# One hybrid encoder step on one core: the down projection's 2x2 block product formed from seven products instead of eight

## The chip, the core and the metric

One NeuronCore of a Trainium2 chip runs the whole step; the other cores are idle. The metric is the device time of one execution in microseconds (us). The engines named below are TensorE (PE in the profile, its weight loads PEld), VectorE (DVE), ScalarE (ACT), GpSimd (POOL) and SyncE (SP), whose queue issues most DMAs.

## The reference, cut to what matters

Two layers process 512 prompt tokens and 32 sample tokens of width 1024. Each layer has a mixer (differential attention and a gated spatial unit), cross-attention to 256 memory tokens, and a feed-forward block with a causal convolution over three tokens. The change is in the last of these:

```python
def conv_ffn(h, hist, w_up, conv_w, conv_b, w_down):
    S = h.shape[1]
    g, up = jnp.split(h @ w_up, 2, axis=-1)          # 1024 -> 2 x 2816
    gp = jnp.concatenate([hist, g], axis=1)
    c = conv_b + sum(conv_w[j] * gp[:, j:j + S] for j in range(CONV_W))
    a = jax.nn.silu(c) * up
    return a @ w_down, gp[:, -(CONV_W - 1):]         # 2816 -> 1024
```

## The kernel before

Features stand on partitions and tokens on the free axis: 546 token columns, which are 512 prompt tokens, 2 columns of padding that carry the sample's convolution history, and 32 sample tokens (`T`, `S0`). One fp32 value is held as a hi part plus a lo part, and each product is three matmuls: hi by hi, hi by lo and lo by hi. `proj_fm` (L263) issues them for each k tile of 128 rows, each in two token parts of 256 and 290 columns (`NSPL`) into two PSUM banks, a and b. Its outputs are `pfg` and `pfu` (gate and up), `pfd` (down), `pq`, `pwo`, `pwc` and `pu` in the other stages.

Weights arrive as a stream of units. `emit_unit` loads a unit into `raw` (three buffers, L130), ACT copies the hi part (L133) and DVE subtracts to get the lo part (L134) into one of four `hl` buffers. `pop` keeps the units up to i + 3 emitted when unit i is used. So the splitting runs ahead of PE by one pair of units.

The feed-forward block of a layer runs in two halves of 11 feature tiles. Per feature tile there is a gate tile and an up tile, each 48 matmuls. DVE scales them by `rbc` (L910, L929), ACT and DVE do the convolution and the activation (L914 to L930), and `split` makes hi and lo of the result `at` (L173, L174). After 11 tiles the down projection runs over eight output tiles `ct`: 33 pairs of matmuls each, then `update_x` adds both banks to the residual `x` (L209). In the second half `after(ct)` follows each of them: in layer 0 `set_h`, which makes the gained hi and lo parts `hx` of the residual (L189, L190) and adds its squares into `ssq` (L196 on ACT, L201 on POOL); in layer 1 `final_x`, which transposes and stores the output.

PSUM has four banks under the tag R, two under S and two under B; `psR2` takes a pair from R, R or S in turn. The order of the instructions on each engine is fixed when the program is built: by place in the program among what is taken to be ready. Engines take their instructions strictly in that order.

## Time and profile before

| | us |
|---|---|
| median of 3 runs | 1721.8 (1720.87 to 1721.93) |
| span of the profiled execution | 1721.5 |
| PE busy | 1700.7 (99%) |
| DVE busy | 996.2 (58%) |
| ACT busy | 728.9 (42%) |
| POOL busy | 220.3 (13%) |

The span runs from the first to the last instruction of the profiled execution. No other time is given for that execution; the median of the runs is 0.3 us above its span. Busy time of PE counts a matmul until its modelled end, so that matmuls overlap: what a matmul costs is the distance from its start to the next one's start, not its duration.

### The profile page before, as it was taken

How to read it: one execution, taken by the hardware profiler on the slowest of the kernel's cores; microseconds unless marked ns; L12 is line 12 of the kernel's file. 1: busy time of each engine (PE TensorE's matmuls, PEld its weight loads, DVE VectorE, ACT ScalarE, POOL GpSimd, SP SyncE). 2: the span in 40 equal slices, each digit the busy share in tenths (PEclk: the TensorE clock that was granted, in tenths of full speed). 3: DMA queues.
4: the chain of work that ended last, by engine and by line, in shares of the span. 5: the costliest groups of instructions: out<-in, count | busy, mean ns of one | idle time of the engine just before them, and what ended most of it. 6: DMA issues, size and time to landing. Idle time of an engine off the chain costs nothing.

```text
span 1721.5 us, 32408 instructions
## 1 busy us (share of the span) xinstructions
PE 1700.7 (99%) x13115; PEld 1641.7 (95%) x13115; DVE 996.2 (58%) x2138; ACT 728.9 (42%) x1485; POOL 220.3 (13%) x624
## 2 busy tenths in 40 slices
PE   7999999999999999999999999999999999999998
PEld 6988899999999999999998888999999999999998
DVE  6778765565466624655367677655555665255642
ACT  5456754455333312333345576445543332133321
POOL 4000014221200000000111000422221000000000
PEclk9999999999999999999999999999999999999999
DMA  5222233442222233223332222243422322333131
GB/s 174 89 86 71 66 102 100 141 130 82 86 79 88 70 88 108 86 68 87 93 117 70 76 69 85 85 130 105 129 81 74 99 62 86 101 94 90 55 115 57
DMA packets 200988, 158.03 MB, mean 92 GB/s; under 512 B 8670, under 2 KB 200038, under 8 KB 200838
## 3 DMA queue, kind: packets, MB, share of 16 engines
q1 hardware_dynamic: 200774, 155.82, 29.8%
q8 instruction: 103, 1.69, 0.4%
q14 instruction: 47, 0.39, 0.1%
q10 hardware_dynamic: 64, 0.14, 0.0%
HBM read 144.83 MB, written 11.10 MB: 91 GB/s over the span
## 4 chain that ended last, share of the span: by engine, by line
PE 95%; ACT 1%; POOL 1%; DVE 1%; issue 1%; SPq 1%; DMA 0%; ACTq 0%; DVEq 0%
PE pfgb L263 8%; PE pfub L263 8%; PE pfdb L263 8%; PE pfua L263 7%; PE pfga L263 7%; PE pfda L263 7%; PE pr L282 4%; PE pr L280 4%; PE pr L281 4%; PE pwob L263 3%; PE pqb L263 3%; PE pwcb L263 3%; PE pwoa L263 3%; PE pwca L263 3%; PE pqa L263 3%; PE pub L263 2%
## 5 line engine op out<-in xcount | busy, mean ns | idle before, releaser
L134 DVE TENSOR_TENSOR hl<-raw,hl 128x1024 fp32r<-128x1024 f32 (+2 forms) x280 | 317.1, 1133 | 278.0 <-ACT hl L133 277.6
L133 ACT CAST hl<-raw 128x1024 fp32r<-128x1024 f32 (+2 forms) x280 | 269.9, 964 | 408.8 <-PE pfdb L263 139.2
L263 PE MATMUL pfgb<-hx,hl 128*128 128x290 f32 x1056 | 269.6, 297 | 0.0
L263 PE MATMUL pfdb<-at,hl 128*128 128x290 f32 x1056 | 269.5, 298 | 0.0
L263 PE MATMUL pfga<-hx,hl 128*128 128x256 f32 x1056 | 269.3, 283 | 0.0
L263 PE MATMUL pfda<-at,hl 128*128 128x256 f32 x1056 | 268.4, 282 | 0.0
L263 PE MATMUL pfub<-hx,hl 128*128 128x290 f32 x1056 | 264.9, 297 | 0.0
L263 PE MATMUL pfua<-hx,hl 128*128 128x256 f32 x1056 | 264.2, 283 | 0.5 <-ACT rbc L253 0.5
L263 PEld LDWEIGHTS pfdb<-at,hl 128*128 128x128 f32 x1056 | 200.4, 190 | 0.1
L263 PEld LDWEIGHTS pfgb<-hx,hl 128*128 128x128 f32 x1056 | 200.4, 190 | 0.0
L263 PEld LDWEIGHTS pfda<-at,hl 128*128 128x128 f32 x1056 | 200.0, 189 | 0.0
L263 PEld LDWEIGHTS pfga<-hx,hl 128*128 128x128 f32 x1056 | 199.6, 189 | 0.0
L263 PEld LDWEIGHTS pfub<-hx,hl 128*128 128x128 f32 x1056 | 198.3, 190 | 0.0
L263 PEld LDWEIGHTS pfua<-hx,hl 128*128 128x128 f32 x1056 | 196.9, 189 | 0.7 <-ACT rbc L253 0.7
L282 PE MATMUL pr<-hl,hx 128*128 128x256 f32 x512 | 147.8, 290 | 2.4 <-DVE hx L190 2.4
L280 PE MATMUL pr<-hl,hx 128*128 128x256 f32 x512 | 147.5, 289 | 1.4 <-DVE vs L305 0.9
L281 PE MATMUL pr<-hl,hx 128*128 128x256 f32 x512 | 147.6, 289 | 0.8 <-DVE hl L134 0.8
L282 PEld LDWEIGHTS pr<-hl,hx 128*128 128x128 f32 x512 | 98.0, 192 | 5.8 <-DVE hx L190 2.8
L281 PEld LDWEIGHTS pr<-hl,hx 128*128 128x128 f32 x512 | 98.3, 192 | 3.6 <-issue 1.7
L280 PEld LDWEIGHTS pr<-hl,hx 128*128 128x128 f32 x512 | 98.0, 192 | 3.7 <-DVE vs L305 1.1
L263 PE MATMUL pwcb<-co,hl 128*128 128x290 f32 x384 | 88.7, 298 | 0.0
L917 DVE SCALAR_TENSOR_TENSOR ct<-gb,cols,ct 128x546 f32<-128x546 f32 x88 | 69.3, 787 | 33.2 <-ACT ct L914 31.6
(360 smaller groups left out, 3312.7 us busy)
## 6 DMA issues: line engine op xcount, KB each, us to landing
raw<-in_w_up_dram SPq DMA_DIRECT2D x80, 512.0 KB
raw<-in_w_down_dram SPq DMA_DIRECT2D x32, 512.0 KB
raw<-in_w_in_dram SPq DMA_DIRECT2D x24, 512.0 KB
raw<-in_w_in_dram SPq DMA_DIRECT2D x32, 256.0 KB
raw<-in_w_out_dram SPq DMA_DIRECT2D x32, 256.0 KB
raw<-in_wq_c_dram SPq DMA_DIRECT2D x16, 512.0 KB
raw<-in_wk_c_dram SPq DMA_DIRECT2D x16, 512.0 KB
raw<-in_wv_c_dram SPq DMA_DIRECT2D x16, 512.0 KB
```

The source lines that it names most:

```text
L133: act.copy(hl[:, 0, 0:n * wc], raw[:, 0:n * wc])
L134: vec.tensor_tensor(out=hl[:, 1, 0:n * wc], in0=raw[:, 0:n * wc], in1=f32(hl[:, 0, 0:n * wc]), op=ALU.subtract)
L263: pe.matmul(out=ps[0 if n0 == 0 else 1][:, 0:nn], lhsT=hl[:, wpart, kk, col * 128:col * 128 + 128], rhs=mv[:, n0:n0 + nn], start=first and ...
L280: pe.matmul(out=out, lhsT=lh(k), rhs=hl[:, 0, k % 4], start=(k == 0), stop=False)
L281: pe.matmul(out=out, lhsT=lh(k), rhs=hl[:, 1, k % 4], start=False, stop=False)
L282: pe.matmul(out=out, lhsT=ll(k), rhs=hl[:, 0, k % 4], start=False, stop=(k == k8 - 1))
L917: vec.scalar_tensor_tensor(out=ct, in0=gb[:, jj:jj + T], scalar=c["cw"][:, jj, f:f + 1], in1=ct, op0=ALU.mult, op1=ALU.add)
```

## The change

The down projection is cut into 2 by 2 blocks: k tiles by even and odd, output tiles by first and second of a pair, tokens by first and second half of 272. Eight block products become seven (the Winograd form of Strassen's algorithm). The sums of weight blocks S1 to S4 are made on POOL in `emit_item`, from the raw weights; the sums of activation blocks T1 to T4 on POOL in `ffn_pair`. Then ACT and DVE make hi and lo parts of the seven weight blocks and of the seven activation blocks. `seven` issues a product after the other, three banks in all, and adds each product's bank to `x` when it ends; later products go on accumulating on the same bank.

The 22 feature tiles are 11 pairs in three parts of 3, 4 and 4 pairs, instead of two halves of 11 tiles. One pair of the next part is computed ahead of each part's down projection, save the last. The padding columns go: 544 columns in two parts of 272, and the sample's first two convolution outputs are corrected by small instructions on POOL and DVE. Weights are loaded in blocks of eight k tiles by 256 columns into two `raw` buffers, and split into eight operands of 4 KB a partition: hi and lo are tiles of their own, and a down block's hi and lo share one. Buffers shrink for it: `skq` and `vs` from two to one, and `cv` shares the one buffer of `ck`.

```diff
-HF = NF // 2
+PARTS = ((0, 3), (3, 7), (7, 11))
...
-T = 546          # tokens on the free axis: 512 prompt, 2 of padding, 32 sample
-S0 = 514         # first sample token
-NSPL = ((0, 256), (256, 290))
+T = 544
+S0 = 512
+TH = T // 2
+NSPL = ((0, TH), (TH, TH))
...
+    blocks, items = [], []
+    ORDER = ("A11", "A12", "S2", "S1", "S3", "S4", "A22")
...
+        def block(tag, loads, nk, seven=False):
+            blocks.append((loads, nk))
+            b = len(blocks) - 1
+            if seven:
+                for it in ORDER:
+                    items.append((tag, b, it))
+            else:
+                for k0 in range(0, nk, 4):
+                    items.append((tag, b, k0))
...
-            for hf in range(2):
-                for f in range(hf * HF, hf * HF + HF, 2):
-                    w = 128 * min(2, hf * HF + HF - f)
...
-                for ct in range(8):
-                    for k0, n in ((0, 8), (8, HF - 8)):
-                        units.append((f"dn{hf}_{ct}", [ks(a["w_down"][l][:, 128 * ct:128 * ct + 128],
-                                                          hf * HF + k0, n)], n, 128))
...
+            def gen(i):
+                two(f"g{i}", a["w_up"][l], [(256 * i, 256)])
+                two(f"up{i}", a["w_up"][l], [(FF + 256 * i, 256)])
+            gen(0)
+            for q, (p0, p1) in enumerate(PARTS):
+                for i in range(p0 + 1, min(p1 + 1, NF // 2)):
+                    gen(i)
+                nk = 2 * (p1 - p0)
+                for j in range(4):
+                    mat = a["w_down"][l][:, 256 * j:256 * j + 256]
+                    block(f"dn{q}_{j}", [(k0, min(4, nk - k0), 0, 256, ks(mat, 2 * p0 + k0, min(4, nk - k0)))
+                                         for k0 in range(0, nk, 4)], nk, seven=True)
...
-        raw = wp.tile([128, 1024], F32, tag="raw", bufs=3, name="raw")
...
-        hl = wp.tile([128, 2, 1024], F32R, tag="hl", bufs=4, name="hl")
-        act.copy(hl[:, 0, 0:n * wc], raw[:, 0:n * wc])
-        vec.tensor_tensor(out=hl[:, 1, 0:n * wc], in0=raw[:, 0:n * wc], in1=f32(hl[:, 0, 0:n * wc]), op=ALU.subtract)
...
+    def load(b):
+        while state["loaded"] <= min(b, len(blocks) - 1):
+            loads, nk = blocks[state["loaded"]]
+            raw = wp.tile([128, 2048], F32, tag="raw", bufs=2, name="raw")
+            rv = raw[:, 0:nk * 256].rearrange("p (k c) -> p k c", c=256)
+            for k0, kn, c0, cn, src in loads:
+                sp.dma_start(out=rv[:, k0:k0 + kn, c0:c0 + cn], in_=src)
+            raws[state["loaded"]] = rv
+            state["loaded"] += 1
+    def hilo(n):
+        return [wp.tile([128, 1024], F32R, tag="hl", bufs=SLOTS, name="hl")[:, 0:n] for _ in range(2)]
...
+    def emit_item(i):
+        tag, b, it = items[i]
+        load(b + 1)
+        raw, nk = raws[b], blocks[b][1]
+        if isinstance(it, int):
+            kn = min(4, nk - it)
+            hi, lo = hilo(kn * 256)
+            src = raw[:, it:it + kn].rearrange("p k c -> p (k c)")
+            act.copy(hi, src)
+            vec.tensor_tensor(out=lo, in0=src, in1=f32(hi), op=ALU.subtract)
+            wt[i] = tuple(v.rearrange("p (k c) -> p k c", c=256) for v in (hi, lo))
...
+        n = nk // 2
+        q = raw.rearrange("p (k e) (c n) -> p e c k n", e=2, c=2)
+        A11, A12, A21, A22 = q[:, 0, 0], q[:, 1, 0], q[:, 0, 1], q[:, 1, 1]
+        def summed(name, in0, in1, op):
+            t = tmp([128, 4, 128], name, tag="c2", bufs=3)[:, 0:n]
+            pool.tensor_tensor(out=t, in0=in0, in1=in1, op=op)
+            sums[name] = t
+        if it == "A11":
+            summed("S1", A21, A22, ALU.add)
+            summed("S2", sums["S1"], A11, ALU.subtract)
+        elif it == "A12":
+            summed("S3", A11, A21, ALU.subtract)
+        elif it == "S3":
+            summed("S4", A12, sums["S2"], ALU.subtract)
+        src = {"A11": A11, "A12": A12, "A22": A22}.get(it)
+        if src is None:
+            src = sums[it]
+        hl = wp.tile([128, 2, 4, 128], F32R, tag="hl", bufs=SLOTS, name="hl")[:, :, 0:n]
+        act.copy(hl[:, 0], src)
+        vec.tensor_tensor(out=hl[:, 1], in0=src, in1=f32(hl[:, 0]), op=ALU.subtract)
         wt[i] = hl
...
+    def cost(i):
+        return 2 if isinstance(items[i][2], int) else 1
+    def prefetch(slots=SLOTS):
+        while state["emitted"] < len(items) and state["held"] + cost(state["emitted"]) <= slots:
+            emit_item(state["emitted"])
+            state["held"] += cost(state["emitted"])
...
+        for i in state.pop("done", ()):
+            state["held"] -= cost(i)
         i = state["popped"]
-        prefetch(i + 4)
+        prefetch()
...
+        state["done"] = range(i, i + n)
...
                 pe.matmul(out=pb[:, 128 * t:128 * t + 128], lhsT=ones, rhs=dg[:, 2 * i + t], start=True, stop=True)
             if i == 1:
                 pe.matmul(out=pb[:, 256:288], lhsT=ones[0:32], rhs=dgs, start=True, stop=True)
-                act.copy(rbc[:, S0:T], pb[:, 256:288])
-            act.copy(rbc[:, 256 * i:256 * i + 256], pb[:, 0:256])
+            act.copy(rbc[:, 256 * i:256 * i + 256 + 32 * i], pb[:, 0:256 + 32 * i])
...
-                                  lhsT=hl[:, wpart, kk, col * 128:col * 128 + 128],
+                                  lhsT=hl[wpart][:, kk, col * 128:col * 128 + 128],
...
-        zs = tmp([32, 256], name, tag="vs" if name == "vs" else "zs", bufs=2)
+        zs = tmp([32, 256], name, tag="vs" if name == "vs" else "zs", bufs=1 if name == "vs" else 2)
...
-        skq = tmp([128, 352], "skq", tag="skq", bufs=2)
+        skq = tmp([128, 352], "skq", tag="skq", bufs=1)
...
-        cv = tmp([128, 2, 128], "cv", tag="cv", bufs=1)
+        cv = tmp([128, 2, 128], "cv", tag="ck", bufs=1)
...
+    def ffn_pair(l, i, rbc, fc, cnt, slots):
...
+            gs = tiny([128, 4], "gs")
+            ge = tiny([128, 2], "ge")
+            pool.tensor_copy(gs[:, 0:2], c["st"][:, :, f])
+            pool.tensor_copy(gs[:, 2:4], gb[:, S0 + 2:S0 + 4])
+            pool.tensor_scalar(out=ge, in0=gs[:, 2:4], scalar1=c["cw"][:, 2, f:f + 1],
+                               scalar2=c["cb"][:, f:f + 1], op0=ALU.mult, op1=ALU.add)
...
+            vec.scalar_tensor_tensor(out=ge, in0=gs[:, 1:3], scalar=c["cw"][:, 1, f:f + 1], in1=ge,
+                                     op0=ALU.mult, op1=ALU.add)
+            vec.scalar_tensor_tensor(out=ct[:, S0:S0 + 2], in0=gs[:, 0:2], scalar=c["cw"][:, 0, f:f + 1],
+                                     in1=ge, op0=ALU.mult, op1=ALU.add)
...
+        h0, h1 = slice(0, TH), slice(TH, T)
+        (sB, sT, sU, sD), d = slots
+        ts = G("t4", [128, 4, TH], "ts")
+        pool.tensor_tensor(out=ts[:, 0], in0=us[0][:, h1], in1=us[0][:, h0], op=ALU.subtract)
+        pool.tensor_tensor(out=ts[:, 1], in0=us[1][:, h1], in1=ts[:, 0], op=ALU.subtract)
+        pool.tensor_tensor(out=ts[:, 2], in0=us[1][:, h1], in1=us[0][:, h1], op=ALU.subtract)
+        pool.tensor_tensor(out=ts[:, 3], in0=us[1][:, h0], in1=ts[:, 1], op=ALU.subtract)
+        dv = sD[:, :, d * TH:d * TH + TH]
+        split(dv[:, 0], dv[:, 1], us[0][:, h0])
+        split(sB[:, 0], sB[:, 1], us[1])
+        for k, t in enumerate((sT, sU)):
+            split(t[:, 0], t[:, 1], ts[:, 2 * k:2 * k + 2].rearrange("p j t -> p (j t)"))
+        bl = {"B11": dv, "B21": sB[:, :, h0], "B22": sB[:, :, h1], "T1": sT[:, :, h0], "T2": sT[:, :, h1],
+              "T3": sU[:, :, h0], "T4": sU[:, :, h1]}
+        return bl, cnt
...
+    SEVEN = (("A11", "B11", 0, True, (0, 0)), ("A12", "B21", 1, True, (0, 0)), ("S2", "T2", 0, False, (0, 1)),
+             ("S1", "T1", 2, True, (1, 1)), ("S3", "T3", 0, False, (1, 1)), ("S4", "B22", 2, False, (0, 1)),
+             ("A22", "T4", 0, False, (1, 0)))
+    def seven(tag, prs, ct):
+        banks = [psR("p7a"), psR("p7b"), psS("p7c")]
+        n = len(prs)
+        for lf, rt, bk, new, (r, h) in SEVEN:
+            w, = pop(tag, 1)
+            ps = banks[bk][:, 0:TH]
+            for k in range(n):
+                m = prs[k][rt]
+                for wpart, part in ((0, 0), (0, 1), (1, 0)):
+                    pe.matmul(out=ps, lhsT=w[:, wpart, k], rhs=m[:, part],
+                              start=new and k == 0 and wpart + part == 0, stop=k == n - 1 and wpart == 1,
+                              skip_group_check=True)
+            xv = x[:, ct + r, h * TH:h * TH + TH]
+            vec.tensor_tensor(out=xv, in0=ps, in1=xv, op=ALU.add)
...
-            if hf == 1:
...
+        pairs[0], cnt = ffn_pair(l, 0, rbc, fc, cnt, slots(0))
+        for q, (p0, p1) in enumerate(PARTS):
+            for i in range(p0 + 1, min(p1 + 1, NF // 2)):
+                pairs[i], cnt = ffn_pair(l, i, rbc, fc, cnt, slots(i))
+            if p1 == NF // 2:
...
-            for ct in range(8):
-                w2 = pop(f"dn{hf}_{ct}")
-                ps = psR2("pfd", cnt)
-                cnt += 1
-                proj_fm(ps, 0, [(w2[0], [(k, av[k][:, 0], av[k][:, 1]) for k in range(8)], True, False),
-                                (w2[1], [(k, av[8 + k][:, 0], av[8 + k][:, 1]) for k in range(HF - 8)], False, True)])
-                update_x(ct, ps)
-                if hf == 1:
-                    after(ct)
+            prs = [pairs.pop(i) for i in range(p0, p1)]
+            for j in range(4):
+                seven(f"dn{q}_{j}", prs, 2 * j)
+                if p1 == NF // 2:
+                    after(2 * j)
+                    after(2 * j + 1)
```

## Rows read from the trace of the kernel before

**Rows 1.** The page's first part: busy time of each engine, share of the span, instructions.
```profile
PE 1700.7 (99%) x13115; PEld 1641.7 (95%) x13115; DVE 996.2 (58%) x2138; ACT 728.9 (42%) x1485; POOL 220.3 (13%) x624
```

**Rows 2.** The page's fourth part: the chain that ended last, by engine.
```profile
PE 95%; ACT 1%; POOL 1%; DVE 1%; issue 1%; SPq 1%; DMA 0%; ACTq 0%; DVEq 0%
```

**Rows 3.** Windows, layer 0: feed-forward tiles, first down half, second down half with gained splits.
```profile
core 0: us, PE busy (x) PEld busy (x) DVE busy (x) ACT busy (x) POOL busy (x), PEclk, DMA share, GB/s
484.00:601.00 117.00, 117.00 (x922) 117.00 (x921) 74.14 (x112) 40.42 (x52) 5.62 (x39) 1.00 0.25 76
601.00:667.40 66.40, 66.40 (x527) 66.40 (x526) 20.79 (x33) 13.37 (x17) 0.00 (x0) 1.00 0.33 98
801.60:868.60 67.00, 67.00 (x530) 67.00 (x529) 26.60 (x43) 22.72 (x31) 9.76 (x11) 1.00 0.34 98
```

**Rows 4.** Timeline of DVE, 560 to 670 us: start, duration, engine, line, operands.
```profile
563.92 0.42 DVE L929 TENSOR_TENSOR up<-pfua,rbc 128x256 f32<-128x256 f32 x1 [0.67 <-PE pfua L263]
...
600.49 0.42 DVE L929 TENSOR_TENSOR up<-pfua,rbc 128x256 f32<-128x256 f32 x1
600.83 0.45 DVE L929 TENSOR_TENSOR up<-pfub,rbc 128x290 f32<-128x290 f32 x1
601.22 0.56 DVE L134 TENSOR_TENSOR hl<-raw,hl 128x384 fp32r<-128x384 f32 x1
601.70 0.72 DVE L930 SCALAR_TENSOR_TENSOR up<-up,ct 128x546 f32<-128x546 f32 x1
603.13 0.73 DVE L174 TENSOR_TENSOR at<-up,at 128x546 fp32r<-128x546 f32 x1 [0.71 <-ACT at L173]
...
608.99 0.42 DVE L209 TENSOR_TENSOR x<-pfda,x 128x256 f32<-128x256 f32 x1
...
667.41 0.42 DVE L209 TENSOR_TENSOR x<-pfda,x 128x256 f32<-128x256 f32 x1
```

**Rows 5.** The chain around 157 us, merged: start, us, what; runs of one width.
```profile
156.55 2.85 PE pua L263 x24
159.41 2.29 PE pub L263 x17
```

**Rows 6.** Timeline of PE at 22 us: 256 columns of `hl` as the moving operand.
```profile
22.02 0.28 PE L282 MATMUL pr<-hl,hx 128*128 128x256 f32 x1
...
22.37 0.28 PE L282 MATMUL pr<-hl,hx 128*128 128x256 f32 x1
```

**Rows 7.** Groups by line and shape, layer 0's feed-forward (465 to 885 us): count, busy, mean ns.
```profile
L134 DVE TENSOR_TENSOR hl<-raw,hl 128x1024 fp32r<-128x1024 f32 x57 | 69.8, 1225 | 106.3 <-ACT hl L133 106.3
...
L134 DVE TENSOR_TENSOR hl<-raw,hl 128x384 fp32r<-128x384 f32 x16 | 8.8, 550 | 0.0
...
L190 DVE SCALAR_TENSOR_TENSOR hx<-x,cols,hx 128x546 fp32r<-128x546 f32 x9 | 7.2, 801 | 2.1 <-ACT hx L189 2.1
...
L134 DVE TENSOR_TENSOR hl<-raw,hl 128x512 fp32r<-128x512 f32 x8 | 5.5, 693 | 2.3 <-ACT hl L133 2.3
```

**Rows 8.** The same groups on ACT: the copies that make the hi parts.
```profile
L133 ACT CAST hl<-raw 128x384 fp32r<-128x384 f32 x16 | 8.2, 514 | 21.7 <-PE pfdb L263 14.8 <-PE pfgb L263 4.0 <-issue 2.9
...
L133 ACT CAST hl<-raw 128x512 fp32r<-128x512 f32 x8 | 5.0, 622 | 13.0 <-PE pfub L263 6.8 <-PE pfgb L263 6.3
```

**Rows 9.** Timeline, all engines, 257 to 265 us: POOL beside DVE.
```profile
257.48 1.37 POOL L201 TENSOR_TENSOR ssq<-ssq,sqx 128x546 f32<-128x546 f32 x1
257.67 2.25 DVE L134 TENSOR_TENSOR hl<-raw,hl 128x1024 fp32r<-128x1024 f32 x1 [0.26 <-ACT hl L133]
258.80 1.18 POOL L163 TENSOR_TENSOR rmt<-rmy 128x2 f32<-128x2 f32 x1
...
264.19 1.37 POOL L201 TENSOR_TENSOR ssq<-ssq,sqx 128x546 f32<-128x546 f32 x1
264.95 0.45 DVE L209 TENSOR_TENSOR x<-pwob,x 128x290 f32<-128x290 f32 x1
```

**Rows 10.** Waits of PE over the whole span: us in total, times, longest.
```profile
PE pr L282 <- DVE hx L190: 2.4, 2, 2.2
```

More of the change, by code (lines that the diff above doesn't have):

```diff
@@ L78, in encoder_step, with ks @@
     xsm = cp.tile([128, 8, 64], F32R, name="xsm")
-    units = []
+    blocks, items = [], []
+    ORDER = ("A11", "A12", "S2", "S1", "S3", "S4", "A22")
     def build_units():
+        def ks(src, k0, n):
+            return src[k0 * 128:(k0 + n) * 128].rearrange("(k p) c -> p k c", p=128)
+        def block(tag, loads, nk, seven=False):
[7 more added lines that the diff above has]
+                    items.append((tag, b, k0))
         for l in range(DEPTH):
             wi = a["w_in"][l]
-            def ks(src, k0, n):
-                return src[k0 * 128:(k0 + n) * 128].rearrange("(k p) c -> p k c", p=128)
             def two(tag, mat, cols):
+                loads = []
                 for k0 in (0, 4):
-                    units.append((tag, [ks(mat[:, c:c + n], k0, 4) for c, n in cols], 4, sum(n for _, n in cols)))
+                    c0 = 0
+                    for c, n in cols:
+                        loads.append((k0, 4, c0, n, ks(mat[:, c:c + n], k0, 4)))
+                        c0 += n
+                block(tag, loads, 8)
             kq = lambda h: two(f"kq{h}", wi, [(512 + 128 * h, 128), (128 * h, 128)])
@@ L100, in build_units @@
                 src = a["w_out"][l][:, 256 * j:256 * j + 256].rearrange("(b q k p) c -> q b p k c", b=2, q=2, p=128)
-                for q in range(2):
-                    units.append((f"wout{j}", [src[q, 0], src[q, 1]], 4, 256))
+                block(f"wout{j}", [(4 * q + 2 * b, 2, 0, 256, src[q, b]) for q in range(2) for b in range(2)], 8)
             for h in range(4):
@@ L138, in prefetch @@
-    def prefetch(upto):
-        while state["emitted"] < min(upto, len(units)):
-            emit_unit(state["emitted"])
+    raws, sums = {}, {}
+    state = {"emitted": 0, "popped": 0, "held": 0, "loaded": 0}
+    SLOTS = 8
+    def load(b):
[7 more added lines that the diff above has]
+            state["loaded"] += 1
@@ L244, in x_stats @@
         rbc = cp.tile([128, T], F32, tag="rbc", name="rbc")
-        pool.memset(rbc[:, SP:S0], 0.0)
         for i in range(2):
@@ L279, in tm_group @@
             hl = w2[k // 4]
-            pe.matmul(out=out, lhsT=lh(k), rhs=hl[:, 0, k % 4], start=(k == 0), stop=False)
-            pe.matmul(out=out, lhsT=lh(k), rhs=hl[:, 1, k % 4], start=False, stop=False)
-            pe.matmul(out=out, lhsT=ll(k), rhs=hl[:, 0, k % 4], start=False, stop=(k == k8 - 1))
+            pe.matmul(out=out, lhsT=lh(k), rhs=hl[0][:, k % 4], start=(k == 0), stop=False)
+            pe.matmul(out=out, lhsT=lh(k), rhs=hl[1][:, k % 4], start=False, stop=False)
+            pe.matmul(out=out, lhsT=ll(k), rhs=hl[0][:, k % 4], start=False, stop=(k == k8 - 1))
     def proj_tm(w2):
@@ L296, in proj_tm @@
             for part in range(2):
-                pe.matmul(out=ps[0:64, 0:256], lhsT=xsm[:, k], rhs=w2[k // 4][:, part, k % 4],
+                pe.matmul(out=ps[0:64, 0:256], lhsT=xsm[:, k], rhs=w2[k // 4][part][:, k % 4],
                           start=(k == 0 and part == 0), stop=(k == 7 and part == 1))
@@ L788, in do_cross_q @@
                 act.activation(out=sq[:, n0:n0 + nn], in_=v, func=AF.Square)
-            act.copy(qs[:, dc], ps[1][:, S0 - 256:T - 256])
+            act.copy(qs[:, dc], ps[1][:, S0 - TH:T - TH])
             q.append(qt)
@@ new lines, in do_ffn, with slots @@
+        pairs, held = {}, {}
+        def slots(i):
+            q = next(j for j, (p0, p1) in enumerate(PARTS) if p0 <= i < p1)
+            tags = held.setdefault(q, list(ATAGS[q]))
+            new = lambda: G(tags.pop(0), [128, 2, T], "at", F32R)
+            res = [new(), new(), new()]
+            d = (i - PARTS[q][0]) % 2
+            if d == 0:
+                held["d"] = new()
+            return res + [held["d"]], d
+        pairs[0], cnt = ffn_pair(l, 0, rbc, fc, cnt, slots(0))
[3 more added lines that the diff above has]
+            if p1 == NF // 2:
@@ L1003, in encoder_step @@
         og = [G("og", [128, 2, T], "og", F32R) for _ in range(4)]
-        for t in og:
-            pool.memset(f32(t[:, :, SP:S0]), 0.0)
         st = {"o": tmp([32, 4, 128], "so", tag="so", bufs=1), "ss": tiny([32, 4], "sss")}
```

107 lines of the change are left out of this document (45 added, 62 removed).

## The prediction

> **What bounds the kernel now.** I read the page's busy times first, then the chain, then windows by stage, then timelines. PE is busy for 99% of the span [rows 1], and 95% of the chain that ended last is PE's [rows 2]. So PE's own time is what a change is paid in, as long as no other engine becomes late. The windows say where there is room: in the feed-forward tiles DVE is busy for 74 of 117 us, in the first down half for 20.8 of 66.4 us, in the second half of layer 0 for 26.6 of 67 us; POOL does nothing in the first and at most 9.8 us in the others [rows 3]. The granted clock is 1.00, its level of 2.4 GHz, in all of them, and DMA is busy a third of the time [rows 3]. The change takes matmuls from PE and puts work on DVE, ACT and POOL in just the stages in which PE has no idle time, so both sides have to be summed.
>
> **What PE gains.** In the first half the updates of two output tiles seven apart start at 608.99 and 667.41 us [rows 4]: 58.42 / 7 = 8.35 us for a tile of 66 matmuls, 126.5 ns each at a mean width of 273. The up tiles give the same: 36.57 us from 563.92 to 600.49 over six tiles of 48 matmuls [rows 4], 127.0 ns. The 32 down tiles so cost 267.1 us. Widths alone: 24 matmuls of 256 columns took 2.85 us and 17 of 290 took 2.29 us [rows 5], 118.8 and 134.7 ns, so 0.47 ns a column, and a 272 column matmul costs 126.0 to 126.3 ns. After the change there are 11 pairs x 4 column blocks x 7 products x 3 = 924 matmuls a layer, 1848 in all instead of 2112: 1848 x 126.0 = 232.8 us. **Minus 34.3 us.** The other 3456 pairs of matmuls of `proj_fm` lose two columns each, 3456 x 0.94 ns = 3.2 us. **Minus 37.5 us** in all.
> One uncertainty pulls down: three matmuls of 256 columns whose moving operand is the weight tile took 0.35 us, 117 ns [rows 6], where those moving the activation took 118.8. Should the new, rounder row length give activations that pace, 1.8 ns x (1848 + 6912) = 16 us more would go. I take nothing of it, because the nearest rows are those of the same operand, and keep it for the low end. For a penalty at the start of each product the bound is small: tiles of 48 matmuls show 127.0 ns with their starts included, against (118.8 + 134.7) / 2 = 126.8 without.
> The Trainium skill (TensorE: Matmul & The Clock Gate, section Back-to-back issue gap) gives columns / 2.4 plus 2.5 ns, 109 ns for 256 columns, where these rows have 118.8. By it the 264 missing products would be worth 30.6 us instead of 33.3.
>
> **What the other engines get.** Per column block with n pairs, per product: one update of 272 columns and one subtraction of n x 128 columns on DVE. Two neighbouring reads of PSUM (L929, 256 columns) start 0.34 us apart, and the 384 column subtraction is followed after 0.48 us [rows 4]; the listed means of the subtractions are longer, since ends overlap, 0.55 us for 384 and 0.69 us for 512 columns [rows 7]. I take 0.35 us for the update, 0.48 for n = 3 and 0.61 for n = 4. POOL makes four sums a block; its two-input sum of 546 columns takes 1.37 us [rows 9], so by columns 0.96 us (n = 3) and 1.28 us (n = 4), an estimate. ACT's copies at 0.51 and 0.62 us [rows 8] leave it half idle.
> The point is that POOL and DVE exclude one another. A sum on POOL runs from 257.48 to 258.85; the subtraction L134 that starts at 257.67 takes 2.25 us instead of 1.23, as if it began at 258.85 [rows 7, 9]. Then a POOL instruction on two elements takes 1.18 us and ends when L134 does [rows 9]. But an update that reads PSUM (L209 at 264.95) takes its usual 0.45 us beside a POOL sum [rows 9]. So one POOL sum costs DVE its length less one update that fits beside it.
> - **n = 3** (PE 63 x 0.126 = 7.9 us a block): DVE 7 x 0.83 = 5.8, POOL 4 x (0.96 - 0.35) = 2.4, together 8.2. Over by 0.3; three blocks of a part have sums of the next running, two layers: **plus 1.8 us** (0 to 10: with nothing beside POOL 9.6, over by 1.7).
> - **n = 4** (PE 84 x 0.126 = 10.6): DVE 6.7 + POOL 3.7 = 10.4. It fits; **plus 0.5** for the unevenness (0 to 14: with nothing beside POOL 11.8, over by 1.2 in 12 blocks).
> - **Last part of layer 0.** Two gained splits (0.80 us each [rows 7]) and two POOL sums of 1.37 us come to each block: 10.4 + 1.6 + 2.0 = 14.0, over by 3.4, in the two blocks that have both. **Plus 5** (2 to 9).
> - **The start of a part.** Products use three banks, and a bank is used again after one product of another: the update of product 0 has to be done when product 1 ends, 2.3 us (n = 3) or 3.0 us (n = 4) after the start. In front of it in DVE's queue may stand the end of the last pair: two scalings 0.72, one product 0.72, three splits at 0.73, up to four weight subtractions 2.0, and three POOL sums of 272 columns, 2.0 us [rows 4, 9]: 7.6 us. If all are in front, PE waits 4.6 to 5.3 us; if the update goes first, nothing. Before, the same chain ended at 603.86, and nobody needed it for eight us. That L134 at 601.22 went between L929 and L930 [rows 4] shows the order fills gaps by readiness, so I take a third, 1.7 us, for six starts: **plus 10** (0 to 30).
> - **Ends.** After the last product two tiles of `x` are fresh instead of one. At the change of layer PE already waits 2.4 us in two waits for the gained split [rows 10], and a second costs 0.80 and its POOL sum more; at the end of the program one more output. **Plus 2.7** (0 to 5).
> - In the tiles, four POOL sums of 272 columns (2.8 us) and 0.8 us of extra splitting a pair come to DVE's 63% busy time [rows 3], with 24 us of PE to hide in: nothing. Lost cover would be seen as PE waiting for banks. The fewer buffers in the mixer: nothing (to plus 4), each serves one head at a time. Weight loads of the down stage go at 98 GB/s [rows 3], and a block ahead remains loaded: nothing. At the start the second block is asked for a little earlier: 1 us either way.
>
> Sum: -37.5 + 1.8 + 0.5 + 5 + 10 + 2.7 = -17.5 us. The profiled span is 1721.5 us and the runs' median 0.3 above it, so 1721.8 - 17.5 = **1704 us**.
>
> **The rivals.**
> - **A: PE stays the bound throughout** (0.14). The order puts each update ahead of the splits, as readiness would have it; only the last part of layer 0 and the ends cost, 2 + 1.5 us. -37.5 + 3.5 = -34: 1688 us, and down to 1672 if the pace of rows 6 comes. For it speaks that the average fits even for DVE; against it, that by place in the program the splits come before the updates.
> - **B: DVE's queue becomes the bound, and the kernel is slower** (0.18). One mechanism: an update stands behind subtractions which stand behind POOL sums, and the bank isn't free. With the upper ends, 30 at the starts, 10 + 14 with nothing beside POOL's sums, 9 in layer 0's last part and 5 at the ends, 68 us are lost: 1721.8 - 37.5 + 68 = 1752 us. It decides from the point at which the added waits of PE pass 37.5 us, 0.22 us a product. For it speaks that the n = 3 blocks are over already; against it, that updates do run beside POOL [rows 9].
> - **C: the two sides cancel** (0.10): waits of 34 to 41 us, 1718.4 to 1725.2 us.
> - That the change doesn't do what it says can be left out: the number of matmuls is read off the loops.
>
> The Trainium skill (SBUF — State Buffer, section Who interferes with whom, and the list ahead of it) calls the port pair of VectorE and GpSimd an exclusive lock for a whole instruction, on VectorE's side for one with two SBUF inputs; this is the ground of B. Rows 9 agree in both directions, 2.25 and 1.18 us.
>
> **How the numbers follow.** The forecast, 1690 to 1718 us, has 0.58. 0.2% of the time, 3.4 us, is about what can be told from no change. Faster: 0.58 + 0.14 = 0.72; within: 0.10; slower: 0.18. The range leaves out the far ends of A and B: from 1684, which takes in A's own 1688, to 1734, where B has half its waits beyond C.
>
> **What would show it.** Right: 1848 matmuls of `seven` starting 126 ns apart; PE's waits for updates of `x` at the starts of parts, some us each, and in the last part of layer 0; subtractions of 512 columns that take over 1 us where a POOL sum lies beside them. For A: no waits of PE on DVE in the down stages. For B: waits of about 0.2 us or more before most products. The gain is wrong if 272 columns cost other than 126 ns; all of it would be wrong if the granted clock fell in the down stages, for which the rows give no price.

## The result, and the profile after

The changed kernel takes 1743.74 us (median of 4 runs, 1742.75 to 1744.05). The kernel before took 1721.87 us beside it (1720.87 to 1723.35). The ratio is 1.0125, 95% interval 1.0111 to 1.0140: slower by 21.9 us where 17.5 us less was forecast, and outside the range of 1684 to 1734. The profiled span of the changed kernel is 1741.0 us, 19.5 us over that of before.

The page of the changed kernel, first the busy times, then the chain that ended last by engine. These answer to [rows 1, 2].

```profile
PE 1681.2 (97%) x12851; PEld 1608.7 (92%) x12851; DVE 1201.2 (69%) x2462; ACT 793.6 (46%) x1621; POOL 501.1 (29%) x860
...
PE 80%; DVE 11%; POOL 2%; ACT 2%; issue 2%; DMA 1%; SPq 1%; ACTq 0%; DVEq 0%; POOLq 0%
```

PE has 264 matmuls less and only 19.5 us less busy time. So its matmuls were slower somewhere, and it was also idle for 59.8 us of the span instead of 20.8. Windows by stage say where. The columns are those of [rows 3]. The stages are, for each layer, the mixer with the cross-attention, then the feed-forward block. First the kernel before:

```profile
0.00:463.20 463.20, 450.72 (x3371) 419.50 (x3372) 295.66 (x751) 247.34 (x596) 98.42 (x235) 1.00 0.33 102
463.20:868.70 405.50, 405.27 (x3191) 405.01 (x3190) 215.18 (x339) 128.45 (x165) 24.57 (x100) 1.00 0.29 87
868.70:1306.60 437.90, 434.51 (x3328) 407.98 (x3328) 275.85 (x710) 232.14 (x568) 82.63 (x201) 1.00 0.30 93
1306.60:1721.50 414.90, 410.21 (x3231) 409.19 (x3230) 209.51 (x339) 120.95 (x156) 14.71 (x88) 1.00 0.28 84
```

Then the changed kernel:

```profile
0.00:486.00 486.00, 461.40 (x3371) 425.54 (x3372) 294.93 (x743) 248.63 (x595) 94.89 (x219) 0.96 0.31 98
486.00:884.00 398.00, 387.76 (x3085) 384.81 (x3084) 320.55 (x505) 159.82 (x235) 169.75 (x231) 1.00 0.28 89
884.00:1341.60 457.60, 443.91 (x3302) 412.71 (x3301) 274.98 (x709) 232.69 (x568) 76.70 (x188) 0.96 0.28 89
1341.60:1741.00 399.40, 388.11 (x3099) 385.63 (x3098) 310.77 (x505) 152.49 (x225) 159.76 (x222) 1.00 0.27 86
```

The two feed-forward blocks, where the change was aimed, got 7.5 and 15.5 us shorter, together **23.0 us**. The two mixer stages got 22.8 and 19.7 us longer, together **42.5 us**; what the change touches there is three smaller buffers, the new weight stream and the two columns less. The mean granted clock there is 0.96 instead of 1.00, with about as many matmuls as before. Smaller windows of the changed kernel show the place in layer 0:

```profile
80.00:100.00 20.00, 15.56 (x114) 13.46 (x112) 16.93 (x56) 10.31 (x24) 1.84 (x7) 0.98 0.30 93
100.00:120.00 20.00, 17.59 (x81) 13.86 (x82) 10.91 (x49) 6.27 (x25) 1.81 (x2) 0.60 0.10 29
```

These are the attention steps of the first heads. PE idles for 4.4 us in the first window, and in the second its clock is at 1.2 GHz for much of the time. The waits of PE over the whole span (line waited for: us in total, times, longest) answer to [rows 10]:

```profile
PE p7a L1039 <- DVE x L1043: 9.0, 7, 2.0
PE p7a L1039 <- DVE hl L196: 7.2, 7, 1.6
...
PE pS L590 <- ACT e L549: 3.7, 5, 1.0
...
PE p7c L1039 <- DVE x L1043: 0.7, 3, 0.4
```

The three lines of `p7` are the waits of the seven products, 16.9 us. `pS` is the score step of the attention, a wait that the kernel before does not have there.

### The profile page after: what moved, and what is told of

Read it like the earlier page. It is cut to its first block, busy times and chain, and to the rows that moved or that the text cites. A ratio compares the mean times of both kernels' runs of the same rounds, so it can differ in the third digit from the quotient of the medians.

```text
span 1741.0 us, 32607 instructions
## 1 busy us (share of the span) xinstructions
PE 1681.2 (97%) x12851; PEld 1608.7 (92%) x12851; DVE 1201.2 (69%) x2462; ACT 793.6 (46%) x1621; POOL 501.1 (29%) x860
## 4 chain that ended last, share of the span: by engine, by line
PE 80%; DVE 11%; POOL 2%; ACT 2%; issue 2%; DMA 1%; SPq 1%; ACTq 0%; DVEq 0%; POOLq 0%
PE pfua L330 6%; PE pfga L330 6%; PE pfgb L330 6%; PE pfub L330 6%; PE p7a L1039 5%; PE pr L348 4%; PE pr L347 3%; PE pr L349 3%; DVE hl L196 3%; PE pwoa L330 3%; PE pwca L330 3%; PE pqb L330 3%; PE pwob L330 3%; PE pqa L330 3%; PE pwcb L330 3%; PE p7c L1039 2%
## 5 line engine op out<-in xcount | busy, mean ns | idle before, releaser
L172 DVE TENSOR_TENSOR hl<-raw,hl 128x1024 fp32r<-128x1024 f32 x208 | 261.0, 1255 | 96.2 <-ACT hl L171 89.1
L171 ACT CAST hl<-raw 128x1024 fp32r<-128x1024 f32 x208 | 218.3, 1051 | 204.8 <-PE pm L348 46.3
L330 PE MATMUL pfua<-hx,hl 128*128 128x272 f32 x1056 | 259.2, 287 | 0.0
L330 PE MATMUL pfub<-hx,hl 128*128 128x272 f32 x1056 | 259.0, 287 | 0.0
L330 PE MATMUL pfga<-hx,hl 128*128 128x272 f32 x1056 | 258.7, 287 | 0.0
L330 PE MATMUL pfgb<-hx,hl 128*128 128x272 f32 x1056 | 257.6, 287 | 0.0
L1039 PE MATMUL p7a<-at,hl 128*128 128x272 f32 x1056 | 149.3, 290 | 16.3 <-DVE x L1043 9.0
L1039 PEld LDWEIGHTS p7a<-at,hl 128*128 128x128 f32 x1056 | 137.5, 188 | 20.0 <-DVE x L1043 10.6
L330 PE MATMUL pwca<-co,hl 128*128 128x272 f32 x384 | 87.5, 289 | 0.0
L330 PE MATMUL pwcb<-co,hl 128*128 128x272 f32 x384 | 87.1, 288 | 0.0
```

The lines of the kernel that those rows point to most:

```text
L171: act.copy(hi, src)
L172: vec.tensor_tensor(out=lo, in0=src, in1=f32(hi), op=ALU.subtract)
L330: pe.matmul(out=ps[0 if n0 == 0 else 1][:, 0:nn], lhsT=hl[wpart][:, kk, col * 128:col * 128 + 128], rhs=mv[:, n0:n0 + nn], start=first and ...
L1039: pe.matmul(out=ps, lhsT=w[:, wpart, k], rhs=m[:, part], start=new and k == 0 and wpart + part == 0, stop=k == n - 1 and wpart == 1, skip_ ...
```

## Experiments

Times are beside runs of the kernel before on the same chip, which took 1721.4 to 1721.9 us. Where one run is given, it stands for differences of more than some 3 us.

### The three buffers alone

Into the kernel before, first all three smaller buffers, then each by itself:

```diff
-        zs = tmp([32, 256], name, tag="vs" if name == "vs" else "zs", bufs=2)
+        zs = tmp([32, 256], name, tag="vs" if name == "vs" else "zs", bufs=1 if name == "vs" else 2)
...
-        skq = tmp([128, 352], "skq", tag="skq", bufs=2)
+        skq = tmp([128, 352], "skq", tag="skq", bufs=1)
...
-        cv = tmp([128, 2, 128], "cv", tag="cv", bufs=1)
+        cv = tmp([128, 2, 128], "cv", tag="ck", bufs=1)
```

All three: 

> The kernel before with the three smaller buffers of the change alone (skq and vs one instead of two, cv in ck's buffer). Theory M: the 43 us that the two mixer and attention stages lost came from these buffers, since they take away the matmuls that stood between the attention's steps; so 1755 to 1768 us, with stretches at the lower granted clock before 180 us and around 1000 us. Rival W: they came from the new weight stream (blocks of 1 MB in two buffers); then 1718 to 1726 us and the clock at 1.00 throughout.

`cv` in the buffer of `ck` alone: 

> The kernel before with cv in the one buffer of ck, nothing else. If M holds I expect this one to carry it, because ck's load then waits for the sample's attention of the head before, and PE was seen to wait for it: 1750 to 1768 us. If another of the three carries it, or W holds: 1718 to 1728 us.

One buffer for `vs` alone: 

> The kernel before with one buffer for vs, nothing else. M with cv as carrier: 1718 to 1727 us. If vs carries it (the second value projection can't end before the sample's attention of head 1): 1750 to 1768 us.

One buffer for `skq` alone: 

> The kernel before with one buffer for skq, nothing else. M with cv as carrier: 1718 to 1725 us. If skq carries it (the keys of the next head wait for the sample's scores): 1750 to 1768 us.

| into the kernel before | us | to before | granted clock |
|---|---|---|---|
| all three | 1766.08 | +44.2 | 0.979 |
| `cv` in the buffer of `ck` | 1765.80 | +43.9 | 0.980 |
| `vs` one buffer | 1749.64 | +27.7 | 0.990 |
| `skq` one buffer | 1723.53 | +1.6 | 0.999 |

The buffers alone cost as much as the mixer lost. The prices don't add up: `cv` by itself costs as much as the three, and `vs`, which was expected to cost at most 5 us if `cv` carries the loss, costs 27.7. With `vs` at one buffer PE waits 3.3 us for ACT (`e`) and 3.2 us for DVE (`rgy`) between 100 and 200 us, where the kernel before has no wait; how the buffer leads to them was not followed in the traces. What follows is about `cv`.

How a buffer of 1 KB a partition costs 44 us is seen in the traces. Windows of 5 us, first the kernel before, then the one with `cv` in the buffer of `ck`:

```profile
90.00:95.00 5.00, 4.75 (x41) 4.47 (x40) 4.60 (x6) 4.91 (x11) 0.88 (x1) 1.00 0.23 51
95.00:100.00 5.00, 5.00 (x42) 4.74 (x42) 4.80 (x25) 2.25 (x8) 0.76 (x3) 1.00 0.61 193
100.00:105.00 5.00, 5.00 (x38) 4.47 (x37) 4.98 (x21) 1.30 (x4) 0.14 (x1) 1.00 0.00 0
```

```profile
90.00:95.00 5.00, 2.44 (x18) 1.80 (x15) 4.91 (x7) 4.48 (x11) 0.82 (x1) 1.00 0.45 126
95.00:100.00 5.00, 2.48 (x5) 1.38 (x5) 4.86 (x33) 1.28 (x7) 0.90 (x3) 0.56 0.26 87
100.00:105.00 5.00, 5.00 (x17) 3.19 (x18) 4.99 (x16) 2.58 (x8) 0.36 (x3) 0.50 0.01 3
```

PE issues 40 matmuls in 5 us before, and 5 to 18 after. DVE is as busy as it was. The timelines (start, us, engine, line, operands, wait) say what went missing. The kernel before, PE and the queue of SP:

```profile
92.19 0.38 PE L451 MATMUL ptrs<-ident,ck 128*128 128x128 f32 x2
92.61 0.38 SPq L448 DMA_DIRECT2D ck<-in_cache_da_k_dram  x1
...
93.06 0.39 PE L280 MATMUL pr<-hl,hx 128*128 128x256 f32 x1 [0.25 <-DVE zs L305]
...
97.81 0.38 PE L525 MATMUL pS<-kT,ql 64*128 64x256 f32 x1
```

And with `cv` in the buffer of `ck`:

```profile
95.80 0.58 PE L523 MATMUL pS<-kT,qT 128*128 128x256 f32 x1 [1.36 <-DVE s L504]
96.66 0.58 PE L525 MATMUL pS<-kT,ql 64*128 64x256 f32 x1 [0.28 <-DVE ql L444]
...
104.43 1.06 PE L572 MATMUL pos<-cv,aTs 128*32 128x128 f32 x4
...
105.52 0.37 SPq L448 DMA_DIRECT2D ck<-in_cache_da_k_dram  x1
...
107.64 0.69 PE L451 MATMUL ptrs<-ident,ck 128*128 128x128 f32 x2 [0.36 <-DMA ck<-in_cache_da_k_dram]
...
108.61 0.58 PE L280 MATMUL pr<-hl,hx 128*128 128x256 f32 x1
```

`ck` of the next head is needed early: its transposes `ptrs` stand in the order ahead of the projection matmuls `pr`, at 92.19 before. When `cv` of this head holds the buffer, the load of `ck` (L448) can start only behind the last reader of `cv`, `pos` at 104.43. So `ptrs` slips to 107.64, and `pr` behind it from 93.06 to 108.61. Those projection matmuls, of the heads to come, had filled PE between the dependent score steps, of which each waits for ACT and DVE. Without them PE waits. From 95.6 us on the granted clock is at 1.2 GHz for 17.07 us, the first of four such stretches in the span, two in each layer; the same step that took 0.38 us takes 0.58.

### The buffers given back to the changed kernel

`cv`, and then `cv` and `vs`, go into the general temporaries of the changed kernel, which have five buffers:

```diff
-        zs = tmp([32, 256], name, tag="vs" if name == "vs" else "zs", bufs=1 if name == "vs" else 2)
+        zs = tmp([32, 256], "vs") if name == "vs" else tmp([32, 256], name, tag="zs", bufs=2)
...
-        cv = tmp([128, 2, 128], "cv", tag="ck", bufs=1)
+        cv = tmp([128, 2, 128], "cv")
```

`cv` alone: 

> The changed kernel with cv alone in the general buffers, vs still in one. In the kernel before, vs alone cost 28 us and cv alone 44. If each acts by itself here too: 1715 to 1732 us, some stretches at the lower clock left. If cv is the whole of it here: 1696 to 1708 us.

Both: 

> The changed kernel with cv and vs in the general buffers of 2.2 KB (tag t, five of them, little used in the mixer) in place of one small buffer each. Theory M: the mixer stages come back to their old time with the clock at its full level, and the rest is as forecast, 1743.7 - 44 = 1700 us (1694 to 1708). Rival: the general buffers become the new wait, or the new weight stream keeps part of the loss: 1712 to 1740 us.

`cv` alone gave 1723.14 us (clock 0.992), both gave 1713.42 us (4 runs, 1710.38 to 1718.04; clock 0.996 in the profiled one, which is the longest). The ratio of the second to before is 0.9947, interval 0.9930 to 0.9963. So 30.3 us of the changed kernel's time were the two buffers, and what is left is faster than before by 8.2 us. That is less than the 23.0 us that the feed-forward blocks gained, and 5 us above the 1694 to 1708 us expected: it lies where the rival had it, by which the general buffers or the new weight stream keep part of the loss. The mixer stages of the profiled run:

```profile
0.00:474.10 474.10, 454.03 (x3371) 420.84 (x3372) 292.31 (x743) 248.32 (x595) 94.09 (x219) 0.99 0.32 101
...
873.90:1315.50 441.60, 432.28 (x3302) 404.22 (x3301) 274.68 (x709) 231.70 (x568) 80.66 (x188) 1.00 0.29 92
```

They are still 10.9 and 3.7 us longer than before. The longest waits of PE that are new there lie in layer 0: 2.4 us for DVE's weight split `hl`, and 1.8 us each for `skq` (ACT), `ws` (POOL) and `z` (DVE). Which part of the change keeps this loss was not separated.

### What the order costs, and what the clock

Into the kernel with `cv` in the buffer of `ck`, and into the kernel before as a control, idle work for PE ahead of the score steps of heads 1 and 2:

```diff
             ps = [psS("pS") for _ in range(2)]
+            for _ in range(12 if h in (1, 2) else 0):
+                pe.matmul(out=ps[0][:, 0:256], lhsT=hx[:, 0, 0, 0:128], rhs=hx[:, 0, 0, 0:256], start=True, stop=True)
```

With the shared buffer: 

> The kernel before with cv in ck's buffer, and with idle work for PE: ahead of each of the eight score steps of heads 1 and 2 twelve more matmuls of 256 columns on operands that are long ready, into the bank of pS, which the step then begins anew. They are 192 matmuls in all, 22.7 us at 118 ns. With cv in ck's buffer the score steps of head 1 stood without projection matmuls from 90 to 106 us, PE waited some 5 us there, and the granted clock was at 1.2 GHz from 95.6 us on for 17.07 us. Theory K, the clock is most of what the shared buffer costs, and it falls because PE has too little to do there: with the fill the clock stays at 2.4 GHz in that stretch, the fill lies partly in the waits, and although there is more to do the stretch from the last projection matmul to the next gets shorter or stays equal; the time is under 1765.8, some 1740 to 1762 us. Theory W, the loss is the waiting for the shared buffer and the order itself, and the clock falls whatever PE does: the stretch gets longer by the fill, the clock is low as before, and the time is 1775 to 1800 us.

Control: 

> The kernel before with the same 192 further matmuls ahead of the score steps of heads 1 and 2, and cv in a buffer of its own. Both theories: nothing waits there and the clock is at 2.4 GHz, so that it takes 1721.8 + 22.7 = 1744.5 us, within 4 us. This is what the fill costs by itself.

The control took 1739.04 us, 17.5 us for the fill, at a clock of 0.999; at least 1740.5 us was expected. With the shared buffer it took 1785.60 us at 0.982, 46.6 us more than the control. So theory K's forecast of a shorter time fails, and the time lies in the range of theory W. But the run tests less than it was meant to. The fill writes the bank of the score step behind it, so it runs after the wait for ACT and not in it, and then at 1.2 GHz itself:

```profile
97.96 2.71 PE L523 MATMUL pS<-hx 128*128 128x256 f32 x12 [0.99 <-ACT e L482]
...
104.98 2.87 PE L523 MATMUL pS<-hx 128*128 128x256 f32 x12 [1.35 <-ACT e L482]
```

In the stretch that was to tell, from `prs` (the projection of the sample's columns) to the next `pr`, both parts can be read. Without fill it runs from 87.44 to 108.61, 21.2 us, of which 13.0 lie at 1.2 GHz. With it, from 87.41 to 112.19, 24.8 us, of which 6.8 lie at 1.2 GHz. The 36 fill matmuls in it, each counted from its start to the next start, are 6.8 us, two thirds of them at 1.2 GHz. So 18.0 us are left without them: 3.2 us less, with most of the slow time gone. Elsewhere the order changed too, and in layer 1 the slow stretches got no shorter (20.5 and 17.1 us).

How much the clock can be at most is read from the four slow stretches of the kernel with the shared buffer, the first of them and their sum:

```profile
95.60:112.67 17.07, 14.79 (x49) 10.00 (x50) 12.17 (x59) 5.25 (x20) 0.79 (x6) 0.50 0.16 48
...
sum 68.28, PE 59.32 PEld 39.67 DVE 46.40 ACT 24.24 POOL 3.80; mean PE 14.83 PEld 9.92 DVE 11.60 ACT 6.06 POOL 0.95
```

PE is busy for 59.3 us there at half the clock. At the full clock that work takes no less than half as long, so by this estimate at most 29.7 of the 43.9 us are the clock's, and at least 14 us are waits and order. In the two long slow stretches with one buffer for `vs` PE is busy for 20.6 of 30.7 us, so that at most 10.3 of its 27.7 us are the clock's. Within these bounds the two shares stay open, and so does K.

### The sums on POOL

In the down stages 17 us of PE's waits are left. Either a split waits for its sum to be made (a delay in the chain), or the sums keep DVE from working (a shared port). From the changed kernel with both buffers given back:

```diff
-            pool.tensor_tensor(out=t, in0=in0, in1=in1, op=op)
-            sums[name] = t
+            sums[name] = in1 if name == "S1" else in0
```

Weight sums left out, the splits read a raw block: 

> As f_both, but POOL's four sums of weight blocks are left out: S1 to S4 are replaced by one of their inputs, so the output is not the reference's; every split and product stays. Theory L: the 20 us in which PE waits in the down stages come from subtractions on DVE that stand behind these sums, so 8 to 16 us less than f_both. Rival: they come from DVE's own load and the starts of parts, so at most 4 us less.

Sums made but not used, with only the last line of that diff: 

> As f_both, with POOL's four sums still made, but the splits read one raw input in place of the sum, so the output is not the reference's. Theory L: the sums' presence on the shared port is what counts, so as f_both, 1706 to 1716 us, with PE's waits in the down stages still over 15 us. Rival Q: it is the wait for a sum's result that counts; then as f_nosum, 1687 to 1694 us.

Sums made by DVE, `vec.tensor_tensor` in place of `pool.tensor_tensor`: 

> As f_both, but the four sums of weight blocks are made on DVE instead of POOL. Theory L (POOL and DVE exclude one another and the update stands behind that): a block of four pairs then has 7 x 0.96 + 4 x 0.6 = 9.1 us of DVE for 10.5 us of PE, so the waits of the down stages nearly go: 10 to 18 us less than f_both, 1693 to 1702 us. Rival D (DVE has too much to do): more work for DVE makes it later, 1712 to 1735 us.

Waits and busy times are those of the profiled runs; that of the first row took 1718.04 us.

| weight sums | us | PE waits of `p7` | DVE busy | POOL busy |
|---|---|---|---|---|
| on POOL | 1713.42 | 16.8 | 1195.3 | 504.3 |
| on POOL, not used | 1718.81 | 18.9 | 1198.6 | 513.0 |
| left out | 1689.59 | none | 1142.2 | 360.2 |
| on DVE | 1692.74 | 1.4 | 1186.5 | 361.6 |

With the sums made for nobody the waits stay; the time is 2.8 us above the range expected, but 0.8 from the profiled run with the sums used. With the sums on DVE, in the chain as before, the waits go. So it is not the delay but POOL's being at work that costs. Without the sums 23.8 us went where 8 to 16 were expected. The two feed-forward blocks then take 384.5 and 390.6 us, some 22 us less than in the changed kernel: more than the 16.9 us of waits that its profile lists. Groups by shape show it. The changed kernel, 512 column blocks (count, busy, mean ns):

```profile
L196 DVE TENSOR_TENSOR hl<-S,hl 128x512 fp32r<-128x512 f32 x64 | 59.2, 935 | 0.8 <-ACT hl L195 0.8
L181 POOL TENSOR_TENSOR S<-raw 128x512 f32<-128x512 f32 x32 | 51.8, 1619 | 12.3 <-DMA raw<-in_w_down_dram 9.7 <-DVE hl L196 1.9
L196 DVE TENSOR_TENSOR hl<-raw,hl 128x512 fp32r<-128x512 f32 x48 | 48.7, 1017 | 0.2
```

The kernel with the sums on DVE:

```profile
L196 DVE TENSOR_TENSOR hl<-S,hl 128x512 fp32r<-128x512 f32 x64 | 42.7, 685 | 0.5 <-ACT hl L195 0.3
...
L196 DVE TENSOR_TENSOR hl<-raw,hl 128x512 fp32r<-128x512 f32 x48 | 33.2, 699 | 0.6 <-ACT hl L195 0.6
L181 DVE TENSOR_TENSOR S<-raw 128x512 f32<-128x512 f32 x32 | 25.3, 790 | 1.1 <-DMA raw<-in_w_down_dram 1.1
```

The same subtraction takes 0.94 to 1.02 us beside POOL's sums and 0.69 without. DVE takes on 96 sums and its busy time falls, from 1195.3 to 1186.5 us. The Trainium skill (SBUF — State Buffer, section Who interferes with whom) has a DVE instruction with two SBUF inputs contend with a POOL instruction that reads SBUF, the later one blocked; the runs agree that they contend, 935 and 1017 against 685 and 699 ns.

The version with the sums on DVE and both buffers given back is faster than both kernels: 1692.74 us (1692.44 to 1693.48, at the low end of what was expected), ratio 0.9834 to before, interval 0.9817 to 0.9850.

### The pace of a matmul

A gate or up matmul took 124.4 ns in the changed kernel instead of 126 ns (below). Three runs ask whether the width did it or where rows start. Rows of `hx` in the kernel before made 560 words long, with parts of 256 and 290 as before (and `skq` with one buffer, so that it stands against 1723.53 us, a single run on another chip):

```diff
-    hx = cp.tile([128, 8, 2, T], F32R, name="hx")
+    hx = cp.tile([128, 8, 2, 560], F32R, name="hx")[:, :, :, 0:T]
```

> The kernel before with one skq buffer (1723.5 us by itself) and hx's rows lengthened from 546 to 560 elements, so that each row begins at a multiple of 64 bytes; widths stay 256 and 290. If the row's start makes the faster pace of 124.5 ns seen for 272 columns, matmuls that move hx get 1 to 2 ns shorter and those that move at (down) stay: 1714 to 1719 us. If it is the equal widths: 1722 to 1725 us.

Parts of 272 and 274 in the kernel before, with its rows of 546 words (the two other places where the split stands follow):

```diff
-NSPL = ((0, 256), (256, 290))
+NSPL = ((0, 272), (272, 274))
```

> The kernel before with its 546 columns in parts of 272 and 274 instead of 256 and 290, nothing else; row starts as before. If equal widths make the faster pace: a pair of matmuls falls from 254.4 to about 250 ns and the time to 1702 to 1712 us. If they don't (rows' starts, or 544 against 546 alone): 1718 to 1724 us.

Rows of `hx` of 546 words in the version with the sums on DVE, parts of 272 as there:

```diff
-    hx = cp.tile([128, 8, 2, T], F32R, name="hx")
+    hx = cp.tile([128, 8, 2, 546], F32R, name="hx")[:, :, :, 0:T]
```

> The kernel with the weight sums on DVE, and with each row of hx lengthened from 544 to 546 words, so that rows start 2184 bytes apart instead of 2176 (34 times 64); nothing else changes, matmuls stay 272 columns wide. In the changed kernel a gate or up matmul of 272 columns started 124.4 ns before the next, where the widths alone, from 118.8 and 134.7 ns, give 126.0 to 126.3. Theory of the place of the rows: rows and column parts that both start at multiples of 64 bytes are read faster, so the pace goes back to the 127.0 ns of the kernel before cut at 272, a pair of matmuls from 249 to 254 ns: over 2112 pairs of gate and up tiles plus 10.6 us, and up to 14 with the other stages that read hx; 1703 to 1707 us. The down matmuls read at, not hx, and stay at 125. Theory of the width: 272 columns have this pace wherever they stand: 124.4 ns and 1692 to 1694 us.

They took 1719.48 us (4.1 less than its control, between the two ranges expected), 1720.20 us (1.2 less than before) and 1698.48 us (1696.96 to 1699.43, so 5.7 more than with rows of 544, again between the two). Equal widths alone bring next to nothing, so the theory of the width falls. The length of the rows moves the pace, in the last run by about half of what the theory of the place expected: 192 matmuls of four tiles take 24.19 us with rows of 546 words, 126.0 ns each.

```profile
632.27 0.43 DVE L975 TENSOR_TENSOR gb<-pfga,rbc 128x272 f32<-128x272 f32 x1
...
656.46 0.43 DVE L975 TENSOR_TENSOR gb<-pfga,rbc 128x272 f32<-128x272 f32 x1
```

That is the pace worked out from widths ahead of the result. The 1 ns that the kernel before is slower than that, at 127.0, remains unexplained; with parts of 272 and 274 its gate and up matmuls are still 127.0 ns apart on average.

## Why the prediction was wrong, point by point

**The step that failed** is "The fewer buffers in the mixer: nothing (to plus 4), each serves one head at a time." The changed kernel's mixer lost 42.5 us, and 30.3 us of the kernel's time came back with two of the three buffers; alone in the kernel before the three cost 44.2. What keeps the rest of the mixer's loss stays open. The reason given is what is wrong. Each buffer serves one head, but the heads overlap: `ck` of the next head is loaded and transposed while `cv` of this one has still to be read, because the projections behind `ptrs` are what fills PE. That is shown for `cv`; for `vs` only the price is. The rows for `cv` were there to be asked. In the kernel before, `ck` of head 1 is transposed at 92.19 us and that of head 2 at 112.33, both ahead of the step that reads `cv` of head 0:

```profile
112.33 0.38 PE L451 MATMUL ptrs<-ident,ck 128*128 128x128 f32 x2
...
114.36 0.62 PE L572 MATMUL pos<-cv,aTs 128*32 128x128 f32 x4
```

In one buffer these can't stand in this order. I looked at the stages in which the change puts work, and not at those from which it takes something.

With -17.5 on record and +42.5 not seen, 1746.8 us would have come out; 1743.74 were measured. The range would have missed it in any case: its upper end, 1734, is put where B has half its waits beyond C, which by the figures of B and C is 1738.6. In the feed-forward blocks the sum held to 5.5 us: -23.0 measured, -17.5 forecast. That is partly luck, for its terms erred more than the sum. With the weight sums left out these blocks are 45.3 us shorter than before, where PE's gain was put at 37.5 for the whole kernel; the sums take some 22 us of it back, where the starts, blocks and the last part were put at 17.3. One by one:

- **Down matmuls, -34.3.** Right. Where PE waits for nothing, in the kernel without the weight sums, the updates of products follow PE. Two products of 12 matmuls each, from the update at 713.61 to the second one after it at 716.62, are 125.4 ns a matmul. By that 1848 take 231.7 us instead of 267.1: -35.4.

```profile
713.61 0.44 DVE L1041 TENSOR_TENSOR x<-p7a,x 128x272 f32<-128x272 f32 x1 [0.40 <-PE p7a L1037]
...
716.62 0.44 DVE L1041 TENSOR_TENSOR x<-p7c,x 128x272 f32<-128x272 f32 x1 [0.15 <-PE p7c L1037]
```

- **Two columns less in 3456 pairs, -3.2.** Too small. In the changed kernel the first gate tiles of two successive pairs are 23.89 us apart, 192 matmuls at 124.4 ns where 126 were expected and 127.0 stood before [rows 4]. In the 4224 matmuls of gate and up tiles alone that is 4224 x 2.6 = 11 us. I had named the possibility ("the new, rounder row length") and left it in the low end. Its size, 1.8 ns a matmul, was near for the gate and up tiles (1.6 ns below 126.0) and too large for the down matmuls (0.6).

```profile
648.75 0.43 DVE L975 TENSOR_TENSOR gb<-pfga,rbc 128x272 f32<-128x272 f32 x1
...
672.64 0.44 DVE L975 TENSOR_TENSOR gb<-pfga,rbc 128x272 f32<-128x272 f32 x1
```

- **The starts of parts, +10.** Too large by the waits of PE. Near the start of the second part of layer 0 PE waits 0.2 us twice, at 718.68 and 723.26, and near that of each last part about 1 us; some 3 us in all. DVE does take the updates ahead of the splits of the last pair: in the first part the first update runs at 586.96, and the first of those splits (L243) at 590.04.
- **Blocks, +1.8 and +0.5.** Too small by the same waits. Inside the blocks of the first two parts PE waited 7.0 us, in one wait of 1.5 or 2.0 us in each part, not in the even surplus that I had summed; one more of 1.6 us lies in the last part of layer 1. In the longest, at 731.68, three sums of POOL stand in a row and each subtraction beside them takes about as long as the sum does. DVE and POOL ahead of it:

```profile
725.68 1.65 POOL L181 TENSOR_TENSOR S<-raw 128x512 f32<-128x512 f32 x1
...
727.40 1.63 POOL L181 TENSOR_TENSOR S<-S,raw 128x512 f32<-128x512 f32 x1
727.80 1.78 DVE L196 TENSOR_TENSOR hl<-raw,hl 128x512 fp32r<-128x512 f32 x1
728.99 1.74 POOL L181 TENSOR_TENSOR S<-raw 128x512 f32<-128x512 f32 x1
...
729.85 1.43 DVE L196 TENSOR_TENSOR hl<-raw,hl 128x512 fp32r<-128x512 f32 x1
731.20 0.43 DVE L1043 TENSOR_TENSOR x<-p7a,x 128x272 f32<-128x272 f32 x1
731.55 0.67 DVE L196 TENSOR_TENSOR hl<-raw,hl 128x512 fp32r<-128x512 f32 x1
```

  The update at 731.20 is the one that PE waits for. The mechanism was told ahead; the two sizes were off. A sum of 512 columns takes 1.36, 1.62 and 1.80 us on POOL by the means of its three groups, 1.29 us at the shortest, where 1.28 was estimated by columns; and the means hide that three of four come together.
- **The last part of layer 0, +5.** Right: 6.3 us of `p7` waits from 830 to 884 us, with the one near its start. The working gives 2 x 3.4 = 6.8, of which 5 was taken without a reason.
- **Ends, +2.7.** Too large, and with a row read wrongly. The two waits of [rows 10] are not at the change of layer but at 24.09 and 27.23 us, ahead of layer 0's first projections. At the change of layer the kernel before waits for no gained split; the changed one does once, 1.3 us at 888.05. From the end of the last down matmul to the end of the span it is 5.6 us where it was 5.4.
- **Covers.** The tiles hide their extra work as forecast, though the four activation sums of a pair took 4.7 us on POOL (by their means) and not 2.8: in the three stretches of gate and up tiles of layer 0 PE is busy for 98.20 of 98.20, 91.70 of 91.70 and 68.80 of 68.80 us. Weight loads were never waited for by PE in the down stages.

Of the rivals, **B** has its mechanism confirmed, PE waiting for updates behind subtractions behind POOL's sums, but at 17 to 22 us of its 68: it doesn't decide, and the slower kernel isn't its doing. The version with the sums on DVE comes near **A**, 1692.7 us for the 1688 that A gave, but not by A's terms: its mixer stages are still 9.2 us longer than before (470.5 and 439.8 us), and the faster gate and up matmuls pay for that. The closing sentence, that all would be wrong if the clock fell in the down stages, looked at the right gauge in the wrong stage: it was 1.00 there and 0.96 in the mixer.

## What to carry to other kernels

Before a buffer is shared or taken away, look up in the trace when its next tenant is first written and when its last reader runs, across iterations of the loop and not within one; if the first comes earlier, the load moves behind that reader, and with it everything that stands behind the load in the order. Dependent steps are cheap as long as independent matmuls stand between them, and their price is seen only where those are gone. Before work is given to POOL because it is idle, count it at DVE's expense as well: here 96 sums cost less on DVE than beside it.
